# First phase of a hybrid decoder trunk: a 128-byte spacer, the vectors on ScalarE's queue, products pass by pass

## The chip, the core and the metric

The kernel runs on one core of one Trainium2 chip. The metric is the device time of one execution in microseconds; several executions are timed and their median is given. The engines of the core work side by side, each through a queue of its own, and wait for each other by semaphores: TensorE (PE) multiplies, VectorE (DVE) and ScalarE (ACT) do elementwise work, GpSimd (POOL) fills constants here, and SyncE (SP) issues nearly all DMAs.

## What is computed

Two layers over a sequence of 1024 tokens of width 1024: a gated linear recurrence (RG-LRU), a dense SwiGLU block, stick-breaking attention, and a second SwiGLU block. The change touches the beginning of the first mixer alone:

```python
def rms_norm(x, g):
    y = xf * lax.rsqrt(jnp.mean(xf * xf, axis=-1, keepdims=True) + RMS_EPS)
    return (y * g.astype(jnp.float32)).astype(x.dtype)
...
u = jnp.einsum("bsd,de->bse", x, w_in) + b_in
gate_branch, rec = u[..., :LRU_WIDTH], u[..., LRU_WIDTH:]
rec = causal_depthwise_conv(rec, conv_w, conv_b)
gl = jnp.einsum("bsnc,gncd->gbsnd", rec_blk, gate_w).reshape(2, bsz, seq, LRU_WIDTH)
```

## The kernel before

Activations lie transposed: 128 features by 512 tokens make a tile, so x is eight slices `d` (`ND`) by two halves `n` (`NH`). Each float32 operand is split into a rounded high part and a rest (`xh`, `xl`; `fh`, `fl`; `whi`, `wlo`), and a product is three passes: high by high, weight-high by low, weight-low by high. `mm3` (L638 to L641) issues the three, one line each.

The **first phase** (L738 to L829) makes four output columns of 128 (`FIRST`: the recurrent columns 8, 9, 10 and the gate column 0) from eight weight slices of 128 by 512. For each k it loads `fr[k]` and `xr[k][0]`, makes `fh`, `fl` (the weights' parts) and `xh`, `xl` (x times the norm's gain, which is a column of the small table `vc`), and runs twelve products, column after column, with three passes each. So 96 products follow for the first half of the tokens. The second half's 96 come from `second(i, ...)`, one column at a time: column 0, then four short products for the norm's sums (L597), then columns 1, 2 and 3. Column 3 with slice k = 7 is the last product of the phase, and it reads `fl7`.

The order of instructions in this phase is that of the code, on all five engines. Ahead of the first product PE runs ten small products of `ident` with itself (L774). On the DMA side, ScalarE's queue carries the first slice of x, and SP's carries `vc`, then `fr0`, `fr1`, `xr1` and so on. ACT's first computing instruction is `x_hi(0, 0)` (L758), in front of which a table is loaded.

**SBUF.** The pool `sp` holds, one behind the other, `fh0` to `fh7`, `fl0` to `fl7` (2048 bytes of a partition each), `sacc0`, `sacc1`, three `sq` and the raw tiles. It is closed at the end of the phase, and the pool `lp` of the recurrence starts at the same byte: `y0` to `y7` of 4096 bytes each, then two buffers `u` of 4160 bytes, then the rest. Both pools are opened with `reuse_waits="tile"`: whoever writes a new tile waits for the last user of the old tiles that lay on its bytes. Weights and x are apart: `xh`, `xl` begin 128 bytes behind a multiple of 256, and the `sp` pool at a multiple of 256.

**PSUM.** `ptile` (L730) hands out eight banks in turn. The first phase holds all eight (four columns by two halves), so the ninth product group, the first of the recurrence, takes the bank of the first column's first half.

The **recurrence** follows from L832 on. Its order on PE, ACT and DVE comes from a planner with costs of its own, and it is the same in both kernels. Its DVE work begins with `u_pad(0)` (L911: three columns of `u` in front, from `nbias`) and `u_half` (L914: `u` from a bank times the norm's factor `rbc`), for two columns; then a weight's low part (L888), the convolution's taps into `rec` (L923), its low part `rl` (L967), a chain of small instructions for the decay (L848 to L871), and the second `rl`. Its PE work begins with 48 products of `xh`, `xl` with `whi`, `wlo` into two banks, and then the gates' products of `rh`, `rl` into `g_ps` (L897 to L907). DVE and PE both take their instructions strictly in the order shown by the program's rows.

Of the kernel before, what the change touches and what calls it, by code (L numbers as in the profile page):

```python
# [9 lines left out]
F32 = mybir.dt.float32  # L10
# [3 lines left out]
AF = mybir.ActivationFunctionType  # L14
# [3 lines left out]
P = 128  # L18
S = 1024
D = 1024  # L20
ND = D // P
# [11 lines left out]
FIRST = (ND, ND + 1, ND + 2, 0)  # L33
# [471 lines left out]
def trunk(  # L505
# [15 lines left out]
    nc = tc.nc  # L521
# [37 lines left out]
    ones = cp.tile([P, 1], F32, name="ones")  # L559
    nc.gpsimd.memset(ones, 1.0)  # L560
    vc = cp.tile([P, P], F32, name="vc")
    tiny = cp.tile([P, 64], F32, name="tiny")
# [4 lines left out]
    xh, xl = [None] * ND, [None] * ND  # L567
# [43 lines left out]
    def all_factors(sums):  # L611
        for step in ("root", "square", "newton", "out"):
            for t in sums:
                getattr(t, step)()
# [23 lines left out]
    def mm3(ps, wh, wl, mh, ml, first, last, **kw):  # L638
        nc.tensor.matmul(ps, lhsT=wh, rhs=mh, start=first, stop=False, **kw)  # L639
        nc.tensor.matmul(ps, lhsT=wh, rhs=ml, start=False, stop=False, **kw)  # L640
        nc.tensor.matmul(ps, lhsT=wl, rhs=mh, start=False, stop=last, **kw)  # L641
# [88 lines left out]
    def ptile(name):  # L730
        turn[0] += 1
        return psl.tile([P, NB], F32, tag=f"a{(turn[0] - 1) % 8}", name=name)

    pa = {j: [ptile("a_ps") for n in range(NH)] for j in FIRST}
# [3 lines left out]
    with ExitStack() as st, tc.manual_schedule(engines={E.PE, E.Activation, E.DVE, E.Pool, E.SP}):  # L738
        sp = st.enter_context(tc.tile_pool(name="sp", bufs=1, reuse_waits="tile"))
        one = lambda name, dt=F32: sp.tile([P, NB], dt, tag=name, name=name)  # L740
        fh = [one(f"fh{k}", F32R) for k in range(ND)]
        fl = [one(f"fl{k}", F32R) for k in range(ND)]
        sacc = [one(f"sacc{n}") for n in range(NH)]
        sq = [one(f"sq{n}") for n in range(3)]
        fr = [one(f"fr{k}") for k in range(ND)]
        xr = [[one(f"xr{d}_{n}") for n in range(NH)] for d in range(ND)]
        f4 = lambda t: t.rearrange("p (t c) -> p t c", t=4)
        nc.scalar.dma_start(xr[0][0], x[0, 0])
        nc.sync.dma_start(vc, table)
        for k in range(ND):  # L750
            nc.sync.dma_start(f4(fr[k]), lru_first[k])
            if k:
                nc.sync.dma_start(xr[k][0], x[k, 0])
        for k in range(ND):
            nc.sync.dma_start(xr[k][1], x[k, 1])

        def x_hi(k, n):
            nc.scalar.activation(xh[k][n], xr[k][n], AF.Copy, scale=vc[:, V_MIX + k : V_MIX + k + 1])  # L758

        def x_lo(k, n):  # L760
            nc.vector.scalar_tensor_tensor(
                xl[k][n], xr[k][n], vc[:, V_MIX + k : V_MIX + k + 1], f32(xh[k][n]), op0=ALU.mult, op1=ALU.subtract
            )

        def x_square(k, n):
            nc.scalar.square(sq[k % 3] if k else sacc[n], xr[k][n])

        def x_add(k, n):
            if k:
                nc.vector.tensor_add(sacc[n], sacc[n], sq[k % 3])  # L770

        bank = pa[FIRST[3]][1]
        for i in range(10):
            nc.tensor.matmul(bank[:, 0:P], lhsT=ident, rhs=ident, start=True, stop=True)  # L774
        for k in range(ND):
            (nc.scalar.copy if k else V.tensor_copy)(fh[k], fr[k])
            x_hi(k, 0)
            x_square(k, 0)
            nc.vector.tensor_sub(fl[k], fr[k], f32(fh[k]))
            x_lo(k, 0)  # L780
            if k:
                x_add(k - 1, 0)
            for t, j in enumerate(FIRST):
                c = slice(t * P, (t + 1) * P)
                mm3(pa[j][0], fh[k][:, c], fl[k][:, c], xh[k][0], xl[k][0], k == 0, k == ND - 1)
        x_add(ND - 1, 0)
        for k in range(ND):
            x_hi(k, 1)
            x_lo(k, 1)
        for k in range(ND):  # L790
            x_square(k, 1)
            x_add(k, 1)

        def second(i, ks):
            for k in ks:
                c = slice(i * P, (i + 1) * P)
                mm3(pa[FIRST[i]][1], fh[k][:, c], fl[k][:, c], xh[k][1], xl[k][1], k == 0, k == ND - 1)

        again = lambda k, dt=F32: sp.tile([P, NB], dt, tag=f"fr{k}", name="again")
        sums = [  # L800
            Factors(sacc[n], again(n, F32R), again(2 + n, F32R), pa[FIRST[3 - n]][1], rbc[n], again(4 + n), rbc[n])
            for n in range(NH)
        ]
        sums[0].hi()
        sums[0].lo()
        second(0, range(ND))
        sums[1].hi()
        sums[1].lo()
        for t in sums:
            t.sums()  # L810
        all_factors(sums)
        sm = lambda name: lc.tile([P, ND], F32, name=name)
        lam = vc[:, V_LAM : V_LAM + ND]
        az, kq, gq, pq, cc, ch = (sm(n) for n in ("az", "kq", "gq", "pq", "cc", "ch"))
        cb = sm("cb")
        nbias = lc.tile([P, ND, 4], F32, name="nbias")
        cw = lambda j: vc[:, V_CW + j * ND : V_CW + (j + 1) * ND]
        bin_rec = vc[:, V_BIN + ND : V_BIN + 2 * ND]
        V.tensor_add(cb, cw(0), cw(1))
        V.tensor_add(cb, cb, cw(2))  # L820
        V.tensor_add(cb, cb, cw(3))
        V.tensor_mul(cb, cb, bin_rec)
        V.tensor_add(cb, cb, vc[:, V_CB : V_CB + ND])
        for j in range(3):
            V.tensor_scalar_mul(nbias[:, :, j], bin_rec, -1.0)
        V.tensor_scalar_mul(tiny[:, 32 : 32 + ND], vc[:, V_FIN : V_FIN + ND], -0.5)
        second(1, range(ND))
        second(2, range(ND))
        second(3, range(ND))  # L829
# [1444 lines left out]
```

## Time and profile before

| | us |
|---|---|
| median of 3 runs | 2161.24 |
| lowest, highest | 2160.73, 2161.38 |
| span of the profiled execution, first to last instruction | 2159.4 |
| median less span (start and end around the instructions; the profiled execution's own total is not listed) | 1.8 |
| DVE busy, share of the span | 1715.8, 79% |
| ACT busy, share of the span | 1099.4, 51% |

The page is of one execution. Its first part gives each engine's busy time; the groups give a line's instructions with mean durations; the timeline gives start, duration, engine, line and tiles of each instruction, and in brackets how long its engine had been idle and what ended that. Starts are microseconds from the first instruction. A product of 128 by 512 takes longer than the distance to the next one, since products overlap: the distance between two starts is what a product costs.

### The profile page before, as it was taken

What the parts mean: (1) busy time and instruction counts of PE and PEld (TensorE: products, weight loads), DVE (VectorE), ACT (ScalarE), POOL (GpSimd) and SP (SyncE); (2) the same over time, 40 slices, a digit from 0 to 9 for tenths busy, and PEclk for the clock granted to TensorE, in tenths of its full rate; (3) what the DMA queues carried; (4) which work ended last, traced back from release to release, by engine and by line L of the source; (5) the groups of instructions that cost most, each with busy time, mean ns of one, the idle gap of its engine ahead of it and who ended that gap; (6) DMA issues with size and microseconds to landing.
All of it is one profiled execution on the core that took longest, in us unless ns stands there. A gap on an engine that the chain in (4) does not pass through costs nothing.

```text
span 2159.4 us, 27027 instructions
## 1 busy us (share of the span) xinstructions
PE 2148.2 (99%) x9954; PEld 1781.6 (83%) x9954; DVE 1715.8 (79%) x2416; ACT 1099.4 (51%) x1793; POOL 29.2 (1%) x40
## 2 busy tenths in 40 slices
PE   9999999999999999999999999999999999999998
PEld 7888888888888888878888888888888888888887
DVE  8978678667777887888888888877967777787887
ACT  6677445344444544565555555544534444454555
POOL 0000020000000000000000000002000000000000
PEclk9999999999999999999999999999999999999999
DMA  4111312344444764444333334532133444467452
GB/s 177 39 49 49 127 39 84 100 139 146 133 160 136 276 198 122 147 141 103 100 97 96 101 88 107 167 139 95 59 117 125 145 140 151 141 233 243 130 161 86
DMA packets 133316, 274.61 MB, mean 127 GB/s; under 512 B 15296, under 2 KB 23872, under 8 KB 133184
## 3 DMA queue, kind: packets, MB, share of 16 engines
q1 hardware_dynamic: 132768, 272.36, 39.6%
q8 instruction: 78, 1.28, 0.2%
q10 hardware_dynamic: 416, 0.52, 0.1%
q14 instruction: 54, 0.44, 0.1%
HBM read 176.88 MB, written 70.78 MB: 115 GB/s over the span
## 4 chain that ended last, share of the span: by engine, by line
PE 96%; DVE 2%; ACT 1%; issue 0%; DMA 0%; POOL 0%; SPq 0%; DVEq 0%; ACTq 0%; POOLq 0%
PE p_ps L641 18%; PE p_ps L639 18%; PE p_ps L640 18%; PE qk_ps L639 4%; PE qk_ps L641 4%; PE qk_ps L640 4%; PE z_ps L2073 3%; PE av_ps L2121 3%; PE wt_ps L2104 3%; PE a_ps L640 3%; PE a_ps L641 3%; PE a_ps L639 3%; PE ob_ps L639 2%; PE ob_ps L640 2%; PE ob_ps L641 2%; PE g_ps L641 1%
## 5 line engine op out<-in xcount | busy, mean ns | idle before, releaser
L639 PE MATMUL p_ps<-vh,wbh 128*128 128x512 f32 x524 | 204.0, 389 | 1.2 <-ACT ta L1738 1.2
L641 PE MATMUL p_ps<-vh,wal 128*128 128x512 f32 x524 | 204.2, 390 | 0.5 <-DVE wal L1133 0.3
L641 PE MATMUL p_ps<-vh,wbl 128*128 128x512 f32 x524 | 204.1, 390 | 0.0
L641 PE MATMUL p_ps<-vh,wcl 128*128 128x512 f32 x524 | 204.0, 389 | 0.0
L639 PE MATMUL p_ps<-vh,wch 128*128 128x512 f32 x524 | 203.9, 389 | 0.0
L640 PE MATMUL p_ps<-vl,wah 128*128 128x512 f32 x524 | 203.9, 389 | 0.0
L640 PE MATMUL p_ps<-vl,wbh 128*128 128x512 f32 x524 | 203.9, 389 | 0.0
L639 PE MATMUL p_ps<-vh,wah 128*128 128x512 f32 x524 | 203.9, 389 | 0.0
L640 PE MATMUL p_ps<-vl,wch 128*128 128x512 f32 x524 | 203.8, 389 | 0.0
L1138 ACT CAST wbh<-sb 128x1024 fp32r<-128x1024 f32 (+2 forms) x69 | 69.8, 1011 | 191.3 <-DVE sb L1122 191.3
L2085 ACT ACTIVATE F<-z_ps 128x512 f32<-128x512 f32 (+3 forms) x188 | 92.1, 490 | 97.6 <-PE z_ps L2073 95.8
L2109 ACT CAST th<-wt_ps 128x512 fp32r<-128x512 f32 x192 | 92.3, 481 | 84.4 <-PE wt_ps L2104 78.1
L2092 DVE TENSOR_TENSOR_SCAN F<-F,unit 128x128 f32<-128x128 f32 (+3 forms) x128 | 104.9, 821 | 33.4 <-ACT F L2085 32.2
L2113 DVE TENSOR_TENSOR tl<-wt_ps,th 128x512 fp32r<-128x512 f32 x192 | 104.9, 546 | 16.6 <-ACT th L2109 16.5
L641 PEld LDWEIGHTS p_ps<-vh,wal 128*128 128x128 f32 x524 | 98.4, 188 | 22.0 <-DVE wal L1133 1.8
L639 PEld LDWEIGHTS p_ps<-vh,wbh 128*128 128x128 f32 x524 | 98.4, 188 | 21.9 <-ACT ta L1738 1.6
L641 PEld LDWEIGHTS p_ps<-vh,wbl 128*128 128x128 f32 x524 | 98.4, 188 | 21.2 <-DVE wbl L1142 0.8
L641 PEld LDWEIGHTS p_ps<-vh,wcl 128*128 128x128 f32 x524 | 98.4, 188 | 20.7 <-DVE wcl L1152 0.4
L640 PEld LDWEIGHTS p_ps<-vl,wbh 128*128 128x128 f32 x524 | 98.4, 188 | 20.5
L640 PEld LDWEIGHTS p_ps<-vl,wah 128*128 128x128 f32 x524 | 98.4, 188 | 20.5
L639 PEld LDWEIGHTS p_ps<-vh,wch 128*128 128x128 f32 x524 | 98.4, 188 | 20.5
L640 PEld LDWEIGHTS p_ps<-vl,wch 128*128 128x128 f32 x524 | 98.4, 188 | 20.5
(436 smaller groups left out, 5496.4 us busy)
## 6 DMA issues: line engine op xcount, KB each, us to landing
raw<-in_ffn_w_in SPq DMA_DIRECT2D x88, 512.0 KB, 3.6
vl<-pd SPq DMA_DIRECT2D x128, 256.0 KB, 3.5
pd<-U SPq DMA_DIRECT2D x90, 256.0 KB, 2.3
raw<-in_ffn_w_out SPq DMA_DIRECT2D x28, 512.0 KB, 4.1
raw<-in_attn_w_qkv SPq DMA_DIRECT2D x24, 512.0 KB, 3.8
kh<-qh SPq DMA_DIRECT2D x64, 128.0 KB, 2.3
kl<-ql SPq DMA_DIRECT2D x64, 128.0 KB, 2.3
acc<-pd SPq DMA_DIRECT2D x28, 256.0 KB, 2.6
```

Of the source, the lines that this page charges most:

```text
L639: nc.tensor.matmul(ps, lhsT=wh, rhs=mh, start=first, stop=False, **kw)
L640: nc.tensor.matmul(ps, lhsT=wh, rhs=ml, start=False, stop=False, **kw)
L641: nc.tensor.matmul(ps, lhsT=wl, rhs=mh, start=False, stop=last, **kw)
L1138: nc.scalar.copy(self.full(self.wb), self.full(self.sb))
L2073: nc.tensor.matmul(ps[:, 0:n], lhsT=lhsT, rhs=rhs, start=i == 0, stop=i == 1)
L2085: nc.scalar.activation(F, Z.pop(c)[:, 0:n], AF.Sigmoid, scale=-SC)
L2092: V.tensor_tensor_scan(rev, rev, unit[:, NB - n :][:, ::-1], 0.0, op0=ALU.mult, op1=ALU.add)
L2104: nc.tensor.transpose(tp[:, c : c + P], F[:, (kb % 4) * P : (kb % 4 + 1) * P], ident)
L2109: nc.scalar.copy(WH[u][:, c:], TP[u][:, c:])
L2113: V.tensor_sub(WL[u][:, c:], TP.pop(u)[:, c:], f32(WH[u])[:, c:])
L2121: nc.tensor.matmul(ps[:, c:], lhsT=VV[q][:, kb, hx], rhs=t.pop(u)[:, c:], start=kb == 4 * G and i == 0, stop=kb == 3 and i == 1,)
```

## The change

Four things change in the first phase. A tile `bent` of 32 floats (128 bytes of a partition) is put in front of `fh0` in the pool `sp` and filled with zeros by GpSimd; nothing reads it. The table `vc` is loaded from ScalarE's queue behind the first slice of x, and no longer from SP's queue. ScalarE then makes one element per partition of `tiny` from `ones` by `AF.Copy`; nothing reads that either. And the twelve products of a slice are issued pass by pass: high by high for all four columns, then weight-high by low for all four, then weight-low by high.

```diff
+        bent = sp.tile([P, P // 4], F32, name="bent")
+        nc.gpsimd.memset(bent, 0.0)
         fh = [one(f"fh{k}", F32R) for k in range(ND)]
         fl = [one(f"fl{k}", F32R) for k in range(ND)]
...
         nc.scalar.dma_start(xr[0][0], x[0, 0])
-        nc.sync.dma_start(vc, table)
+        nc.scalar.dma_start(vc, table)
+        nc.scalar.activation(tiny[:, 59:60], ones, AF.Copy, scale=ones)
...
-            for t, j in enumerate(FIRST):
-                c = slice(t * P, (t + 1) * P)
-                mm3(pa[j][0], fh[k][:, c], fl[k][:, c], xh[k][0], xl[k][0], k == 0, k == ND - 1)
+            for i, (w, m) in enumerate(((fh, xh), (fh, xl), (fl, xh))):
+                for t, j in enumerate(FIRST):
+                    nc.tensor.matmul(
+                        pa[j][0], lhsT=w[k][:, t * P : (t + 1) * P], rhs=m[k][0],
+                        start=k == i == 0, stop=k == ND - 1 and i == 2,
+                    )
```

Line numbers behind the phase grow by three to six. In the rows below, `DMAHW..` is the landing of a DMA, and `PE_49`, `DVE_49`, `Activation_49`, `Pool_49` are the engines' own counters.

The first place is ACT's queue at the very start, before:

```order
L748 DMA xr0_0_189<-in_x 128x512
L758 ACT_TABLE_LOAD [waits DMAHW1_49]
L758 ACTIVATE xh0_0_93<-xr0_0_189,vc_80 128x512 [waits DMAHW0_49]
L766 ACTIVATE sacc0_176<-xr0_0_189 128x512
L776 CAST fh1_161<-fr1_182 128x512 [waits DMAHW3_49]
```

and in the changed kernel:

```order
L750 DMA xr0_0_191<-in_x 128x512
L751 DMA vc_80<-in_table 128x128
L752 ACT_TABLE_LOAD
L752 ACTIVATE tiny_81<-ones_78 128x1 [waits Pool_49]
L761 ACTIVATE xh0_0_93<-xr0_0_191,vc_80 128x512 [waits DMAHW2_49,DMAHW0_49]
L769 ACTIVATE sacc0_178<-xr0_0_191 128x512
```

The table load stood behind the wait for `vc`; now it waits for nothing, and `x_hi(0, 0)` has both waits for its data.

The second place is PE at the first slice, behind the ten products of `ident`, before:

```order
L639 MATMUL a_ps_144<-xh0_0_93,fh0_160 128x512 [waits DVE_49,Activation_49]
L640 MATMUL a_ps_144<-xl0_0_109,fh0_160 128x512 [waits DVE_49]
L641 MATMUL a_ps_144<-xh0_0_93,fl0_168 128x512
L639 MATMUL a_ps_146<-xh0_0_93,fh0_160 128x512
L640 MATMUL a_ps_146<-xl0_0_109,fh0_160 128x512
```

and in the changed kernel:

```order
L788 MATMUL a_ps_144<-xh0_0_93,fh0_162 128x512 [waits DVE_49,Activation_49]
L788 MATMUL a_ps_146<-xh0_0_93,fh0_162 128x512
L788 MATMUL a_ps_148<-xh0_0_93,fh0_162 128x512
L788 MATMUL a_ps_150<-xh0_0_93,fh0_162 128x512
L788 MATMUL a_ps_144<-xl0_0_109,fh0_162 128x512 [waits DVE_49]
```

The product that needs `xl0` was the second and is now the fifth.

The third place is DVE at the seam to the recurrence, where `u_583` (`u_586` in the changed kernel) is the recurrence's first buffer `u`, and `a_ps_144` to `a_ps_147` are the banks of the first phase's columns 0 and 1. Before:

```order
L826 TENSOR_SCALAR tiny_81<-vc_80 128x8
L911 COPY u_583<-nbias_467 128x3 [waits DVE_49]
L914 TENSOR_TENSOR u_583<-a_ps_144,rbc0_83 128x512 [waits PE_49]
L914 TENSOR_TENSOR u_583<-a_ps_145,rbc1_84 128x512 [waits PE_49]
L911 COPY u_587<-nbias_467 128x3
L914 TENSOR_TENSOR u_587<-a_ps_146,rbc0_83 128x512
L914 TENSOR_TENSOR u_587<-a_ps_147,rbc1_84 128x512 [waits PE_49]
L888 TENSOR_TENSOR wlo_577<-raw_568,whi_576 128x1024 [waits DMAHW3_49]
```

and in the changed kernel:

```order
L832 TENSOR_SCALAR tiny_81<-vc_80 128x8
L917 COPY u_586<-nbias_470 128x3 [waits DVE_49,PE_49]
L920 TENSOR_TENSOR u_586<-a_ps_144,rbc0_83 128x512
L920 TENSOR_TENSOR u_586<-a_ps_145,rbc1_84 128x512
L917 COPY u_590<-nbias_470 128x3
L920 TENSOR_TENSOR u_590<-a_ps_146,rbc0_83 128x512
L920 TENSOR_TENSOR u_590<-a_ps_147,rbc1_84 128x512
L894 TENSOR_TENSOR wlo_580<-raw_571,whi_579 128x1024 [waits DMAHW3_49]
```

The order is the same, but the first copy into `u` now waits for PE, and the multiplications behind it no longer do.

## Prediction

> **What bounds the kernel now.** I read the page's first part and its chain first.
>
> ```profile
> span 2159.4 us, 27027 instructions
> PE 2148.2 (99%) x9954; PEld 1781.6 (83%) x9954; DVE 1715.8 (79%) x2416; ACT 1099.4 (51%) x1793; POOL 29.2 (1%) x40
> PE 96%; DVE 2%; ACT 1%; issue 0%; DMA 0%; POOL 0%; SPq 0%; DVEq 0%; ACTq 0%; POOLq 0%
> ```
>
> PE is never idle for long, and the chain that ended last is PE for 96% of the span. So whatever PE gains or loses in the first phase stands at the end unless PE waits for something later that did not move with it; all later work hangs on PE, directly or through DVE. Averages say no more than that: the change must be read at its own place. The timeline of the first 8 us:
>
> ```profile
> 0.74 0.40 SPq L749 DMA_DIRECT2D vc<-in_table  x1
> 0.74 0.41 ACTq L748 DMA_DIRECT2D xr<-in_x  x1
> 0.87 0.10 POOL L560 MEMSET ones<- 128x1 f32 x1
> 0.91 0.10 POOL L563 MEMSET tiny<- 128x1 f32 x1
> 1.19 0.90 SPq L751 DMA_DIRECT2D fr<-in_lru_first  x2
> 1.45 4.63 PE L774 MATMUL a_ps<-ident 128*128 128x128 f32 x20 [1.45 <-POOL ident masks.py:199]
> 3.68 1.28 ACT L758 ACT_TABLE_LOAD   x1 [3.68 <-DMA vc<-in_table]
> 4.57 0.43 DVE L776 CAST fh<-fr 128x512 fp32r<-128x512 f32 x1 [3.34 <-DMA fr<-in_lru_first]
> 4.97 0.72 ACT L758 ACTIVATE xh<-xr,vc 128x512 fp32r<-128x512 f32 x1
> 5.75 0.80 PE L639 MATMUL a_ps<-xh,fh 128*128 128x512 f32 x1
> 6.53 0.29 PEld L640 LDWEIGHTS a_ps<-xl,fh 128*128 128x128 f32 x1 [0.50 <-DVE xl L761]
> 6.99 0.73 ACT L758 ACTIVATE xh<-xr,vc 128x512 fp32r<-128x512 f32 x1 [0.27 <-DMA xr<-in_x]
> 7.12 0.55 PE L641 MATMUL a_ps<-xh,fl 128*128 128x512 f32 x1
> 7.51 0.40 PE L639 MATMUL a_ps<-xh,fh 128*128 128x512 f32 x1
> ```
>
> The table load waits for `vc` and then holds `xh` until 4.97. The first product starts at 5.75, where the small `ident` products end as well, and the second waits 0.50 for `xl`. Products take 0.80 at first and 0.40 from 7.51 on: PE runs at half rate until about 7.4, that is for 6.0 us from its first instruction at 1.45.
>
> Next, what a product costs, from starts in PE's timeline in this phase and behind it (the last row is of the view by windows; its last two numbers are the share of the DMA engines and GB/s):
>
> ```profile
> 34.57 0.40 PE L641 MATMUL a_ps<-xh,fl 128*128 128x512 f32 x1
> 35.97 0.39 PE L640 MATMUL a_ps<-xl,fh 128*128 128x512 f32 x1
> 52.24 0.40 PE L641 MATMUL a_ps<-xh,fl 128*128 128x512 f32 x1
> 52.47 0.39 PE L639 MATMUL a_ps<-xh,whi 128*128 128x512 f32 x1
> 64.04 0.39 PE L639 MATMUL g_ps<-rh,whi 128*128 128x512 f32 x1
> 64.27 0.39 PE L640 MATMUL g_ps<-rl,whi 128*128 128x512 f32 x1
> 72.88 0.39 PE L639 MATMUL g_ps<-rh,whi 128*128 128x512 f32 x1
> 36.00:52.40 16.40, 16.40 (x72) 13.32 (x71) 13.53 (x26) 6.66 (x8) 0.00 (x0) 1.00 0.10 33
> ```
>
> From 7.51 to 34.57 there are 116 distances, 0.2333 us each; from 35.97 to 52.47 there are 71, 0.2324 each; from 52.47 to 64.27, in the recurrence, 52 of 0.2269. So the first phase's products, whose weights and x lie 128 bytes apart modulo 256, cost 0.006 more than the recurrence's, where they lie alike.
>
> Last, DVE at the seam to the recurrence:
>
> ```profile
> 42.27 0.17 DVE L911 COPY u<-nbias 128x3 f32<-128x3 f32 x1
> 42.34 1.28 DVE L914 TENSOR_TENSOR u<-a_ps,rbc 128x512 f32<-128x512 f32 x2
> 43.60 1.28 DVE L914 TENSOR_TENSOR u<-a_ps,rbc 128x512 f32<-128x512 f32 x2
> 44.80 1.22 DVE L888 TENSOR_TENSOR wlo<-raw,whi 128x1024 fp32r<-128x1024 f32 x1
> 45.94 6.44 DVE L923 SCALAR_TENSOR_TENSOR rec<-u,vc,rec 128x1024 f32<-128x1024 f32 x5
> 52.29 1.22 DVE L967 TENSOR_TENSOR rl<-rec,rh 128x1024 fp32r<-128x1024 f32 x1
> 53.43 1.28 DVE L923 SCALAR_TENSOR_TENSOR rec<-u,vc,rec 128x1024 f32<-128x1024 f32 x1
> 54.62 0.16 DVE L848 SCALAR_TENSOR_TENSOR az<-vc 128x8 f32<-128x8 f32 x1
> 61.17 1.22 DVE L967 TENSOR_TENSOR rl<-rec,rh 128x1024 fp32r<-128x1024 f32 x1
> 71.54 0.68 DVE L914 TENSOR_TENSOR u<-a_ps,rbc 128x512 f32<-128x512 f32 x1
> ```
>
> None of these rows carries an idle time in brackets: from 42.27 on DVE works without a hole, ten microseconds ahead of the end of PE's phase at 52.24 plus 0.40. PE uses that work soon: the second `rl` ends at 62.39 and is read by the product at 64.27, 1.9 us later; the multiplication that ends at 72.22 frees the bank that the product at 72.88 writes, 0.65 later. These two are the cover that DVE has.
>
> **The change part by part.** The sums are made in the time of this execution (span 2159.4, which lies 1.8 below the median of 2161.24; that rest is taken as unchanged).
>
> *Start.* `vc` goes out on ACT at about 1.19, where `fr0` goes out now. `fr0` was used at 4.57, so by that row `vc`, which is smaller but shares the engines with two slices, is there at about 4.6; the ends are 4.0 (2.9 after issue, as `vc` took on SP's queue: 0.74 to 3.68) and 6.4 (the 5.2 that the later slices took, by the rows of DMA issues below). With the table loaded meanwhile, `xh` takes 0.72 and ends near 5.3. PE gains nothing there: it is in its small products until 5.75. I take 5.75 for the first product; the later end of `vc` would make it 7.2. The spacer's fill on POOL stands ahead of `ident`: POOL's fills start 0.04 apart, so it moves PE's small products by 0.03 to 0.1.
>
> ```profile
> fr<-in_lru_first SPq DMA_DIRECT2D x7, 256.0 KB, 5.2
> vc<-in_table SPq DMA_DIRECT2D x1, 64.0 KB, 2.9
> ```
>
> *Pass by pass.* Four products need only `xh` and `fh`, so the 0.50 wait for `xl` goes. But PE is at half rate there: a product there costs between 0.39 (7.12 to 7.51, in which the rate changed) and twice 0.2267; I take 0.43. Three products from 5.75, the first of 0.59 with its weights (as from 6.53 to 7.12), bring the fourth to 7.2, where it was 7.51. Gain 0.3, between 0 and 0.5. Later slices have their data long before PE comes to them (`xh` of slice 1 ends at 7.72; PE comes to it twelve products after 5.75, behind 9), so the order of passes does nothing more.
>
> *Spacer, on products.* It brings weights and x to the same place modulo 256, as in the recurrence. At 0.2269, 116 distances give 0.74 and 71 give 0.39: with the few left out, 1.2 in all. The bounds are 0 and this.
>
> The Trainium skill ("TensorE: Matmul & The Clock Gate", section "Step-by-step: what each phase is for") says that PE reads weights and moving data through two independent SBUF ports, so that loading weights takes nothing from a running product. By it the spacer would bring 0 and the sum would end 1.2 higher. The two distances above speak for the spacer, so I keep 1.2.
>
> So the last product of the phase starts at 52.24 - 0.3 - 1.2 = 50.8 and ends near 51.2.
>
> *Spacer, on memory: the term that decides.* `fh` and `fl` are sixteen times 2048 bytes, `y0` to `y7` eight times 4096: both 32768. So now `u` begins exactly where `sacc0` did, and its earlier owners are tiles that DVE itself used last. With 128 bytes in front, the last 128 bytes of `fl7` slide under `u`. `fl7` is read by the last product of the phase, so the copy into `u` has to wait for PE's last product; the order shows that this copy gains a wait for PE and that the multiplications behind it lose theirs, as behind a wait that covers them. The copy moves from 42.27 to about 51.25: DVE stands still for 9 us, and everything above moves by 9.0. ACT waits for these `u` too.
>
> PE then meets DVE three times. (a) The first product of the recurrence takes the bank that the first multiplication reads: done at 51.25 + 0.07 + 0.69 = 52.0, where PE would be at 51.0. PE waits 1.0. (b) 48 products later PE is at 62.9 and goes on with the first `rh`, `rl`; the second `rl` ends at 62.39 + 9.0 = 71.4. The product that stood at 64.27 starts at 71.45: 7.2 later than before, after 6.2 us of idle PE. (c) The multiplication at 71.54 moves to 80.5 and ends at 81.2; the product that stood at 72.88 starts at 81.25, though PE alone would be there at 80.05. That is 8.4 later than before: 9.0 of delay less the smallest cover of 0.65. Behind this point DVE, busy 79% of the span, can catch up, and nothing makes PE catch up, so 8.4 stays.
>
> *Half rate again.* The end of the trace shows what PE's clock does when it has nothing to do:
>
> ```profile
> 2152.29 0.28 PE L1583 MATMUL ob<-we,vl 128*128 128x256 f32 x1
> 2156.00:2157.80 1.80, 0.00 (x0) 0.00 (x0) 0.00 (x0) 0.00 (x0) 0.00 (x0) 1.00 1.03 343
> 2157.80:2159.40 1.60, 0.00 (x0) 0.00 (x0) 0.00 (x0) 0.00 (x0) 0.00 (x0) 0.51 0.01 3
> ```
>
> The granted clock falls to half at 2157.8, 5.2 us after the last product. The wait in (b) is 6.2, so I expect the fall within it, and then half rate for a while behind 71.45; at the start it lasted 6.0. Each product then costs 0.20 more (0.43 for 0.2269). At 6.0 us that is 14 products, 2.8; at 4.0 it is 9, 1.9. Of it 1.2 lies under the wait in (c), which PE no longer has to sit out. So 0.7 to 1.6 is added; I take 1.1 (5 us).
>
> Sum: 8.4 + 1.1 = 9.5, and 2161.24 + 9.5 = **2170.7**.
>
> The Trainium skill (same page, section "What's actually happening") says that the clock is judged in free-running windows of 3413 ns: one idle window halves it, one busy window restores it. This trace agrees: from 7.4 to 2157.8 are 630.0 such windows. By that rule a wait of 6.2 holds a whole idle window in about four executions of five, and the return takes 4 to 7 us, so executions would differ by 1 to 2 us among themselves.
>
> **Rivals.** *The clock doesn't fall* in the wait: 8.4, so 2169.6. For it: the trace shows one such fall only, and 6.2 is little more than its 5.2. *The spacer doesn't change the products' cost*: the phase ends 1.2 later, DVE and PE with it: 2171.9. For it: the first phase is also the one with the most DMA traffic and the busiest DVE, which could cost PE the 0.006; against it, the phase's second part costs 0.2324 at a DMA share of 0.10. *The wait is covered*: the new wait on the copy could stand only for the products that the multiplications waited for anyway, which are done by 42.3; or DVE's delay could stay below the cover. The deciding point is a start of the copy at 44.1 (42.27 plus 1.9, less little): ahead of it PE never waits, and the change brings its gains alone, 0.3 + 1.2: 2159.7, not slower. Against it stands the arithmetic of the bytes. *The start is late*: `vc` at 6.4 costs up to 1.4 less what half rate hides, so 2171.5 to 2172.
>
> **How the numbers follow.** Forecast 0.57, clock keeps 0.19, products keep their cost 0.10, late start 0.05, wait covered 0.09. The first four lie between 2168.5 (8.4 less an error of 0.4 in each of two covers, and 0.3 for the spread of runs) and 2172.8 (8.4, 1.6 for the clock, the spacer's 1.2 lost, and 0.3 again). The range is **2168.5 to 2172.8**; the covered wait at 2159.7 is left out with its 0.09. A measurement of this kernel tells about 0.2% (4.3 us) from no change: the first four are slower by more than that, the covered wait falls within it, and nothing in the change can bring 4.3. Faster 0.01, same 0.09, slower 0.90.
>
> **What would show it.** In the profile of the changed kernel: the distance of products in the first phase 0.227; the copy into `u` (L917) with some 9 us of idle time in brackets, released by PE at about 51; the product of the second `rl` near 71.5 with about 6 us of idle time, released by DVE L973; products of 0.8 us behind it if the clock fell; the wait for `vc` ended by 5.0. I am wrong if L917 starts near 42, or if PE has made up the delay by 100 us.

## The result, and the profile after

| | before | changed |
|---|---|---|
| median of 5 runs each, us | 2161.16 | 2172.82 |
| lowest, highest | 2160.73, 2161.38 | 2172.03, 2173.52 |
| span of the profiled execution | 2159.4 | 2170.4 |

The changed kernel is slower by 11.7 us: the ratio is 1.0053, with a 95% interval of 1.0042 to 1.0063. The forecast was 2170.7 with a range of 2168.5 to 2172.8, so the median lies at the range's upper bound, 0.02 beyond it as the figures stand. The profiled execution's own time is 2172.21, which is near the low end of the five.

The page of the changed kernel, its first part and its chain:

```profile
span 2170.4 us, 27031 instructions
PE 2149.7 (99%) x9954; PEld 1782.4 (82%) x9954; DVE 1715.7 (79%) x2416; ACT 1098.0 (51%) x1794; POOL 29.2 (1%) x41
PE 93%; DVE 3%; ACT 1%; DMA 1%; issue 1%; SPq 0%; DVEq 0%; ACTq 0%
```

The same number of products keeps PE busy for 1.5 us more, which cannot make 11. The chain shows where to look: PE's share falls from 96% to 93% and DVE's rises by a point, so a stretch has come in where PE is not what ends last. The waits of the changed kernel between 36 and 110 us, PE's first and then DVE's largest (the sum, how often, the longest):

```profile
PE g_ps L640 <- DVE rl L973: 6.1, 1, 6.1
PE g_ps L639 <- ACT rh L935: 0.9, 1, 0.9
PE a_ps L639 <- DVE u L920: 0.9, 1, 0.9
DVE u L917 <- PE a_ps L641: 10.3, 1, 10.3
```

Before the change PE had no wait there that the same view lists. Now the rows of the timeline behind these four, in order of time:

```profile
51.41 0.39 PE L641 MATMUL a_ps<-xh,fl 128*128 128x512 f32 x1
51.84 0.17 DVE L917 COPY u<-nbias 128x3 f32<-128x3 f32 x1 [10.29 <-PE a_ps L641]
52.66 0.50 PE L639 MATMUL a_ps<-xh,whi 128*128 128x512 f32 x1 [0.85 <-DVE u L920]
65.41 0.50 PE L639 MATMUL g_ps<-rh,whi 128*128 128x512 f32 x1 [0.89 <-ACT rh L935]
70.71 1.22 DVE L973 TENSOR_TENSOR rl<-rec,rh 128x1024 fp32r<-128x1024 f32 x1
71.98 0.80 PE L640 MATMUL g_ps<-rl,whi 128*128 128x512 f32 x1 [6.08 <-DVE rl L973]
72.58 0.63 PE L641 MATMUL g_ps<-rh,wlo 128*128 128x512 f32 x1
76.84 0.47 PE L639 MATMUL g_ps<-rh,whi 128*128 128x512 f32 x1
77.15 0.40 PE L640 MATMUL g_ps<-rl,whi 128*128 128x512 f32 x1
81.08 0.68 DVE L920 TENSOR_TENSOR u<-a_ps,rbc 128x512 f32<-128x512 f32 x1
```

A copy of three columns, 0.17 long, waits 10.29 us until the phase's last product (51.41 plus 0.39) is done. DVE's next work moves with it: the second `rl` from 61.17 to 70.71 and the multiplication from 71.54 to 81.08, both by 9.54. PE meets that delay at 71.98 after 6.08 idle, and the products behind stand 0.43 apart (72.58 to 76.84, ten distances) instead of 0.227. The view by windows shows the clock there (length, then busy time and count of PE, PEld, DVE, ACT, POOL, then the granted clock, DMA share and GB/s):

```profile
63.33:66.74 3.41, 1.69 (x7) 0.83 (x5) 3.00 (x14) 1.99 (x2) 0.00 (x0) 1.00 0.00 0
66.74:70.15 3.41, 0.00 (x0) 0.00 (x0) 2.83 (x18) 0.00 (x0) 0.00 (x0) 0.50 0.00 0
70.15:73.57 3.42, 1.59 (x4) 1.30 (x5) 3.35 (x9) 0.00 (x0) 0.00 (x0) 0.50 0.00 0
73.57:76.98 3.41, 3.41 (x10) 2.64 (x9) 3.41 (x6) 2.52 (x2) 0.00 (x0) 0.50 0.00 0
76.98:80.39 3.41, 3.41 (x17) 2.77 (x16) 3.34 (x4) 3.03 (x5) 0.00 (x0) 1.00 0.45 154
```

The clock is at half from 66.74 to 76.98, of which PE has work for the last 5.0 us.

To place the loss I use one measure throughout: the **lead**, the start of a product less the start of the same product before the change (a positive lead is late). In the changed kernel it is -0.83 at the phase's last product (51.41 against 52.24), 7.71 at the product of `rl` (71.98 against 64.27), 10.20 when the kernel before stands at 78 us, and 10.66 at the last product of all. So nearly all of the loss arises within 26 us.

The beginning came out unlike the forecast:

```profile
1.20 0.45 ACTq L751 DMA_DIRECT2D vc<-in_table  x1
1.67 1.28 ACT L752 ACT_TABLE_LOAD   x1 [1.67 <-PEq L2268]
4.34 0.43 DVE L779 CAST fh<-fr 128x512 fp32r<-128x512 f32 x1 [3.11 <-DMA fr<-in_lru_first]
5.42 0.72 ACT L761 ACTIVATE xh<-xr,vc 128x512 fp32r<-128x512 f32 x1 [2.15 <-DMA vc<-in_table]
6.19 1.20 PE L788 MATMUL a_ps<-xh,fh 128*128 128x512 f32 x4 [0.39 <-ACT xh L761]
7.22 1.07 PE L788 MATMUL a_ps<-xl,fh 128*128 128x512 f32 x4
```

The table is loaded early, as meant, but then ACT stands idle for 2.15 us until `vc` has landed. The first product starts at 6.19, 0.44 later than before. The four products of `xl` wait for nothing.

### The profile page after: what moved, and what is told of

Same layout as the page of the kernel before. It is cut to its first block, busy times and chain, and to the rows that moved or that the text cites. A ratio compares the mean times of both kernels' runs of the same rounds, so it can differ in the third digit from the quotient of the medians.

```text
span 2170.4 us, 27031 instructions
## 1 busy us (share of the span) xinstructions
PE 2149.7 (99%) x9954; PEld 1782.4 (82%) x9954; DVE 1715.7 (79%) x2416; ACT 1098.0 (51%) x1794; POOL 29.2 (1%) x41
## 3 DMA queue, kind: packets, MB, share of 16 engines
q8 instruction: 78, 1.28, 0.2%
## 4 chain that ended last, share of the span: by engine, by line
PE 93%; DVE 3%; ACT 1%; DMA 1%; issue 1%; SPq 0%; DVEq 0%; ACTq 0%
PE p_ps L641 18%; PE p_ps L639 18%; PE p_ps L640 18%; PE qk_ps L639 4%; PE qk_ps L641 4%; PE qk_ps L640 4%; PE z_ps L2079 3%; PE av_ps L2127 3%; PE wt_ps L2110 3%; PE ob_ps L639 2%; PE ob_ps L640 2%; PE ob_ps L641 2%; PE a_ps L639 2%; PE a_ps L640 2%; PE a_ps L641 2%; PE g_ps L640 1%
```

## The experiments

The theory was: the 128 bytes push the end of `fl7` under the recurrence's first `u`, so a copy on DVE waits for PE's last product; that wait, and half rate behind it, are the whole loss. The rivals were a late start (through `vc`), the pass order, and the spacer's effect on PE itself. Eleven kernels ran, in three groups; each is compared with the kernel before in runs of its own group.

| kernel | median, us | runs | before | ratio, 95% interval | lead at 52, at 78, at the end |
|---|---|---|---|---|---|
| `e1_u_moved` | 2161.53 | 11 | 2161.35 | 1.0001 [0.9992, 1.0010] | -0.59, -0.61, 0.39 |
| `e2_spacer_alone` | 2171.25 | 5 | 2161.35 | 1.0046 [1.0033, 1.0058] | -1.28, 8.97, 9.31 |
| `e3_no_spacer` | 2161.32 | 11 | 2161.35 | 1.0001 [0.9992, 1.0010] | -0.37, -0.34, -0.52 |
| `e4_spacer_u_moved` | 2160.57 | 11 | 2161.35 | 0.9997 [0.9988, 1.0006] | -1.32, -1.34, -0.75 |
| `e5_vc_on_sp` | 2161.04 | 11 | 2161.23 | 0.9999 [0.9990, 1.0008] | -1.38, -1.37, -0.27 |
| `e8_spacer_256` | 2161.46 | 10 | 2161.23 | 1.0001 [0.9992, 1.0010] | -0.16, -0.15, 0.63 |
| `e6_pe_busy` | 2172.86 | 4 | 2161.23 | 1.0055 [1.0041, 1.0069] | -0.76, 9.19, 10.99 |
| `e7_after_again` | 2172.25 | 4 | 2161.23 | 1.0053 [1.0039, 1.0067] | -0.69, 10.13, 10.49 |
| `e10_pe_busy_24` | 2172.44 | 5 | 2161.22 | 1.0051 [1.0039, 1.0064] | -0.82, 9.09, 10.73 |
| `e11_after_third` | 2172.68 | 5 | 2161.22 | 1.0052 [1.0040, 1.0065] | -0.98, 10.00, 10.31 |
| `e9_spacer_64` | 2160.77 | 10 | 2161.22 | 0.9999 [0.9989, 1.0008] | -1.25, -1.25, -0.96 |

**Is it the bytes under `u`?** The changed kernel with 128 bytes put in front of the first `u` and 128 behind the second, so that `u` begins where `sacc0` did and the rest on a multiple of 256. The products and the start are unchanged.

```diff
+        lp.tile([P, 32], F32, name="gap0")
...
+            if len(U) == 2:
+                lp.tile([P, 32], F32, name="gap1")
```

> The changed kernel, with 128 bytes left free between the y buffers and the u buffers (and 128 more behind the two u, so that everything behind keeps its place modulo 256): u no longer lies on fl7. Theory (the wait of the copy into u for the phase's last product costs the time): the copy starts near 41 without a wait, PE never waits 6 us, the clock stays full, and of the changed trace only the lead of about 0.85 us at the phase's end is left: 2160.3 us. Rival (the cost lies in the new order of passes, in the start or in the moved table vc): 2170 us or more. Rival (only the clock's half rate costs, the wait itself is covered): about 2169.

The copy in the timeline of this kernel:

```profile
41.73 0.17 DVE L920 COPY u<-nbias 128x3 f32<-128x3 f32 x1
```

No idle time stands in brackets, the view of waits lists none for PE between 36 and 110 us, and the 11 us are gone: 2161.53 against 2172.82 (runs of different groups; the kernel before agrees within 0.2 in them). The wait is the cause. The gain that should have been left, about 1 us, is not there: the lead is only -0.59 at the phase's end, and later waits use it up.

**Does the spacer do it alone?** The kernel before with `bent` and its fill, and nothing else.

```diff
+        bent = sp.tile([P, 32], F32, name="bent")
+        nc.gpsimd.memset(bent, 0.0)
```

> The kernel before with the 128-byte spacer and its fill alone. Theory: products of the first phase at 0.227 us, the copy into u waits about 10 us for PE, PE waits about 6 us for the second rl: as slow as the changed kernel, 2172 to 2173.5 us. Rival (pass order and start carry the cost): close to the time before, 2160 to 2161.2.

```profile
51.38 0.17 DVE L913 COPY u<-nbias 128x3 f32<-128x3 f32 x1 [10.22 <-PE a_ps L641]
```

PE's longest wait in it between 36 and 110 us:

```profile
PE g_ps L640 <- DVE rl L969: 6.1, 1, 6.1
```

The same waits, and 9.9 us of loss (2171.25 less 2161.35). So neither the queue of `vc` nor the pass order is needed for it. The median lies 0.75 under the range that was expected. Two differences of its trace from that of the changed kernel point the same way: the copy stands at 51.38, 0.46 earlier, and half rate ends at 74.91, 2.1 earlier.

**And the rest without the spacer?** The changed kernel without `bent`.

```diff
-        bent = sp.tile([P, P // 4], F32, name="bent")
-        nc.gpsimd.memset(bent, 0.0)
```

> The changed kernel without the spacer: vc on ScalarE's queue, the early table load and the order pass by pass are left. Theory: no wait of the copy for PE, products at 0.233 us, first product near 6.2 and the wait for xl gone: a lead of about 0.5 us, of which the norm's sums may take a part: 2160.6 to 2161.2 us. Rival (these parts carry the cost): 2165 us or more.

It takes as long as the kernel before. Its first product also starts at 6.19, the distance of products stays at 0.2333 from 35.54 to 51.87, and up to 100 us the lead never goes beyond -0.62. The median lies 0.1 above the range that was expected. The other edits together are worth nothing that can be measured.

**What the spacer is worth without its wait.** The kernel before with `bent`, `gap0` and `gap1`.

> The kernel before with the spacer, and with u moved away from fl7 as in e1. Theory: the spacer's gain alone, 187 products 0.006 us cheaper, 1.2 us, of which up to 0.5 is given back where the norm's sums wait for DVE: 2160.0 to 2160.5 us. Rival (the lower cost of products came from something else than the spacer): products at 0.233 and 2161.2 us.

PE's first and last products of the phase's second part in this kernel (70 distances):

```profile
35.04 0.39 PE L640 MATMUL a_ps<-xl,fh 128*128 128x512 f32 x1
50.92 0.39 PE L641 MATMUL a_ps<-xh,fl 128*128 128x512 f32 x1
```

(50.92 - 35.04) / 70 = 0.2269, where the kernel before had 0.2324. The lead of -1.32 is not the spacer's alone: -0.27 stands at the fourth product already. From there to the norm's sums it goes to -1.04, 0.11 is lost at the sums, and behind them it goes from -0.93 to -1.32. So the products themselves bring 1.16, the 1.2 that the prediction took for them, and the lead lasts until later waits take half. The median is 0.8 us lower, the lowest of the eleven kernels, but the interval of the ratio holds 1.

**Is it the place of the weights modulo 256, or any displacement?** The kernel before with a spacer of 256 bytes, `gap0` of 256 and no `gap1`; then one with a spacer of 64 bytes, `gap0` of 64 and `gap1` of 192.

```diff
+        bent = sp.tile([P, 64], F32, name="bent")
+        nc.gpsimd.memset(bent, 0.0)
...
+        lp.tile([P, 64], F32, name="gap0")
```

> The kernel before with a spacer of 256 bytes and u moved by as much: everything lies elsewhere, but weights and x are 128 bytes apart modulo 256 as before. Theory (the place modulo 256 sets a product's cost): products of the first phase at 0.233, 2161.2 to 2161.5 us. Rival (any shift or the added tile helps): 0.227 and about 2160.5 us, as e4.

> The kernel before with a spacer of 64 bytes, and the places behind the weights made up to 256 bytes so that u and the tiles behind it lie as before. Weights and x then stand 64 bytes apart in a window of 256 (128 in the kernel before, 0 with the 128-byte spacer). If any distance but 0 costs, products keep their 0.233 us and the first phase is as long as before (lead within 0.2 us at 50 us). If only 128 costs, the pitch is 0.227 and the lead at 50 us is 1.2 to 1.4 us. Total 2160.5 to 2161.6 either way.

With 256 bytes the products cost the same as before, (52.08 - 35.81) / 70 = 0.2324, and the lead stays at -0.14 to -0.16 from the fourth product to the phase's last:

```profile
35.81 0.39 PE L640 MATMUL a_ps<-xl,fh 128*128 128x512 f32 x1
52.08 0.40 PE L641 MATMUL a_ps<-xh,fl 128*128 128x512 f32 x1
```

With 64 bytes, weights and x then 64 apart, they cost 0.2290 (34.96 to 50.99):

```profile
34.96 0.40 PE L640 MATMUL a_ps<-xl,fh 128*128 128x512 f32 x1
50.99 0.40 PE L641 MATMUL a_ps<-xh,fl 128*128 128x512 f32 x1
```

So what counts is where the weights lie modulo 256, and not that something was displaced: 128 apart costs 0.0055 a product more than 0 apart, and 64 apart 0.002, between the two outcomes that had been set down. No run moved x, so the distance between weights and x and the place of the weights by itself are not told apart. The lead of -1.25 with 64 bytes looks as large as that of `e4_spacer_u_moved`, but 0.50 of it is there at the fourth product already (0.27 there), from a start that differs from run to run.

**What `vc` on ScalarE's queue costs.** `e1_u_moved` with `vc` back on SP's queue; table load and pass order stay.

```diff
-        nc.scalar.dma_start(vc, table)
+        nc.sync.dma_start(vc, table)
```

> As e1 (the whole change, u moved off fl7), but with vc back on SP's queue ahead of the first weights. Theory (vc behind x on ScalarE's queue lands late, near 5.4, and sets the first product at 6.2 to 6.4): xh starts near 3.9, the first product at 5.8 where PE's small products end, and the time is 0.4 to 1.0 us under e1: 2160.3 to 2161.0. Rival (the late start is hidden by the norm's sums): the same as e1, 2161.5.

The beginning of this kernel:

```profile
3.91 0.72 ACT L761 ACTIVATE xh<-xr,vc 128x512 fp32r<-128x512 f32 x1 [1.14 <-DMA xr<-in_x]
5.80 1.87 PE L788 MATMUL a_ps<-xh,fh 128*128 128x512 f32 x4
```

`xh` starts 1.5 us sooner than with `vc` on ScalarE's queue (5.42). The median of 2161.04 lies 0.5 under that of `e1_u_moved`, which ran in another group; both intervals hold 1, so the times alone don't tell the two apart. The other price is at the norm's sums. The waits of the changed kernel between 28 and 37 us hold a row that the kernel with `vc` on SP's queue doesn't have:

```profile
PEld a_ps L597 <- DVE again L593: 1.2, 2, 0.7
```

ACT starts its chain of squares later, so `again` is later (33.45 against 32.61), and the sums on PE wait for it: from the last product ahead of the sums to the second behind them it is 2.25 us (33.29 to 35.54), against 1.38 here and 1.40 before. So the new place of `vc` takes back some 0.85 of what the spacer had gained by then.

**Is half rate a term of its own?** The changed kernel with products of `ident` by `ident` into the first gate's bank, ahead of its first product, so that PE is busy through most of its wait; 34 of them, then 24. Beside each the changed kernel itself ran once more.

```diff
+            for _ in range(34 if eg == (0, 0) and n == 0 else 0):
+                nc.tensor.matmul(PS[eg, n][:, 0:P], lhsT=ident, rhs=ident, start=True, stop=True)
```

> The changed kernel with 34 added products of ident with itself (128x128, overwritten by what follows) ahead of the first gate product, some 7 us of PE work at full rate in front of its long wait. Theory (the half rate behind the wait is part of the loss): PE's wait shrinks to below 1 us, the clock stays full, the wait for u's bank near 81.8 ends the delay instead: 1.2 to 1.8 us faster than the changed kernel, about 2171.2. Rival (the half rate lies under DVE's work and costs nothing): the same as the changed kernel, 2172.8. If the added products outlast the wait, 2173 or more.

> The changed kernel again, word for word, so that e6 has it on the same chip. Theory: 2172 to 2173.5 us, the clock at half rate for 7 to 10 us around the wait for the second rl.

> The changed kernel with 24 (not 34) idle products of ident by ident ahead of the first gate product. If the half rate after the wait is a term of its own of about 1 us, the clock stays at 1.00 from 60 to 84 us, the product that used to wait for the second rl starts at about 72.0, the lead lost by 78 us is 9.0 to 9.3 us instead of the 10.2 of the changed kernel, and the median is about 1 us under that of the changed kernel in the same call (about 2171.8 against 2172.8). Rival: the median stays within 0.4 us of the changed kernel's, as with 34 products; then what the clock gives back early is lost again at the later waits for transfers (980, 1533, 2010 us), which would be seen as steps of the lead there.

> The changed kernel once more, beside the kernel with the 24 products: 2172.0 to 2173.5; clock at half rate for two or three stretches of 3.41 us after 66 us; lead lost by 78 us 10.1 to 10.3 us, by the end 10.4 to 10.7.

The windows of the kernel with 24, and its wait for the second `rl`:

```profile
63.70:70.00 6.30, 6.30 (x53) 5.90 (x51) 5.34 (x31) 1.99 (x2) 0.00 (x0) 1.00 0.00 0
70.00:73.00 3.00, 1.11 (x5) 0.86 (x5) 2.90 (x8) 0.00 (x0) 0.00 (x0) 1.00 0.00 0
73.00:77.00 4.00, 4.00 (x19) 3.15 (x18) 4.00 (x8) 2.53 (x2) 0.00 (x0) 1.00 0.01 4
```

```profile
PE g_ps L640 <- DVE rl L975: 1.9, 1, 1.9
```

The clock stays full in both, and the lead at 78 us is 9.19 and 9.09, against 10.20, 10.13 and 10.00 in three traces of the changed kernel. At its place half rate costs 0.8 to 1.1 us in the changed kernel. In `e2_spacer_alone` it costs less: half rate ended at 74.91, after 3.4 us of PE's work. Set against the delay of the copy, since that differs between traces, the lead at 78 us is 0.45 and 0.49 less with full clock, 0.42 to 0.63 more in the changed kernel, and 0.15 less in `e2_spacer_alone`, so some 0.3 there. But the totals did not follow: 2172.86 against 2172.25 with 34 products, where 1.2 to 1.8 us less was expected, and 2172.44 against 2172.68 with 24, where about 1 us less was. The steps of the lead show where it went. Around 980 us a product waits for a transfer, in the kernel with 34:

```profile
PE z_ps L2081 <- DMA kl<-ql: 1.2, 1, 1.2
```

In the kernel before this wait is 0.2. There the lead grows by 0.99 and 0.76 in the two kernels with full clock, and by 0.27, 0.24 and 0.48 in the three traces with half rate. A second such place is at about 2010 us: 0.45 and 0.59 are lost there with full clock, and 0.05, 0.22 and 0.47 are won with half rate. The two places together take back more than the whole gain. Why they fall out so was not found, and with so few traces it can be chance; the runs of one of these kernels also lie 0.7 to 3.1 us apart.

## Why the prediction was right, point by point

*The copy waits for PE's last product, and the spacer's 128 bytes do it.* Right: with the bytes moved the wait is gone (`e1_u_moved`), and the spacer alone brings it (`e2_spacer_alone`). The rival of a covered wait fell with the first trace. Only the size was a little small: the copy was put at 51.25 and came at 51.84, so DVE lost 9.54 instead of 9.0.

*The start.* This is the term that had the wrong sign, when what it does at the norm's sums is counted in: a gain of 0.3 was forecast, and 0.52 gained at the fourth product less 0.85 lost at the sums is a loss of 0.33. `vc` was to be there at 4.6; it was used at 5.42 (the bounds were 4.0 and 6.4), so the first product came 0.44 later and not at 5.75. The 0.50 wait for `xl` went, as forecast. In this trace the clock was also full from 5.30 on, where it was from 7.44 before, so the fourth product started at 6.99 instead of 7.51 in spite of the late start. The record of the clock begins at these times; before them the length of the products tells of half rate. Whether the change has a part in that is open: the clock became full between 4.5 and 5.8 in the seven traces with `vc` on ScalarE's queue, and between 5.4 and 7.4 in the other six. That the fourth product came earlier than forecast is luck, as far as anything here shows. "The order of passes does nothing more" held. That a late `vc` also reaches the sums through ACT, for 0.85, was not in the prediction at all; less the 0.2 by which the fourth product beat its forecast (-0.5 instead of -0.3), it is the 0.6 by which the copy was late.

*The spacer on products.* Right: 0.2267 from 35.54 to 51.41, and 0.2269 in `e4_spacer_u_moved`; without spacer, or with 256 bytes, the old distance. The rival that products keep their cost is out. The Trainium skill's rule of two independent ports ("TensorE: Matmul & The Clock Gate", section "Step-by-step: what each phase is for") would have given 0 here; the measured 0.0055 a product speaks against it for these operands. No run shows why the place costs, or that it is the loading of weights that costs it.

*PE meets DVE three times.* (a) 0.85 idle, forecast 1.0. (b) 6.08 idle and 71.98, forecast 6.2 and 71.45; a wait of 0.89 for `rh` just ahead of it, at 65.41, was not foreseen and cost nothing beside it, since the product of `rl` could not start sooner. (c) With half rate PE did not have to wait, as the prediction had it; with full clock it did, 0.9, and the lead was 9.1: the 9.54 of delay less 0.65 of cover is 8.9, where the forecast had 8.4.

*Half rate again.* The fall came, in every trace with that wait unfilled (four of four, `e2_spacer_alone` among them), so the rival that the clock stays is out. PE worked at half rate for 5.0 us, as taken, and the cost at the place is 0.8 to 1.1, the 1.1 of the sum (in `e2_spacer_alone`, with 3.4 us of such work, some 0.3). What it adds to the total could not be told from nothing, as said above.

The sum by the trace: 8.9 and 1.3 (in this trace: 10.20 - 8.9) by 78 us, 0.46 at later waits, 0.34 between the last product and the end, which is the 11.0 of the spans; the profiled execution lies 0.6 under its median. The forecast's 9.5 lacked 0.7 in the first 78 us, mostly the late copy, and counted nothing behind it. It had said that behind that point nothing makes PE catch up; it also held that nothing more is lost, which is not so by half a microsecond. The range left little room for that: the terms of its upper bound add up to 2172.74.

## What to carry to other kernels

Ahead of moving a tile in a pool whose bytes a later pool takes over, write down for each later tile which old tile will then lie under it and who used that last: here 128 bytes cost 11 us, because the tile newly beneath is last read by PE, ten microseconds after DVE was ready to write there. The price of such a wait is the delay of the waiting engine less the smallest time by which its later results are ahead of their use; here that gave 8.9, and half rate and later waits came on top. An edit with several parts is worth taking apart: its one part of value, the spacer, came to 0.8 us under the kernel before once 128 bytes more kept `u` in its place, which these runs could not tell from nothing.

## What the runs showed of the hardware

A product's cost depends on where its weights lie in a window of 256 bytes of a partition, with x always at one place: 0.2324 to 0.2333 us at 128 bytes apart, 0.2290 at 64, 0.2267 to 0.2269 at 0.

The clock falls without an idle stretch of its own. It steps at intervals of 3.41 us (half rate lasted 10.24 here, three of them, and 6.83 in `e2_spacer_alone`, two). The stretch from 63.33 to 66.74 had PE busy for 1.69 of 3.41 and was followed by half rate; the one from 70.15 to 73.57, busy for 1.59, did not bring the full clock back. In `e7_after_again` a stretch with 2.16 busy kept it:

```profile
62.99:66.40 3.41, 2.16 (x9) 1.23 (x7) 3.07 (x13) 1.96 (x2) 0.00 (x0) 1.00 0.00 0
66.41:69.82 3.41, 0.00 (x0) 0.00 (x0) 2.87 (x18) 0.03 (x1) 0.00 (x0) 1.00 0.00 0
```

So for the fall about half a stretch of work decides, and the end of the kernel before, where 1.56 kept the full clock, says that the bound is not a sharp one in busy time. The rise takes more: in the kernel before, PE was busy with its small products for 2.58 of the 3.41 us up to 4.03, and the products of 0.80 behind that show half rate still; in `e1_u_moved` 3.01 busy up to 4.52 was enough. The Trainium skill ("TensorE: Matmul & The Clock Gate", section "What's actually happening") asks for one idle window of 3413 ns; the length agrees, but by that rule the clock would have stayed until 70.15 here. Where in its stretch a wait begins differs from execution to execution, and with it when half rate begins: 66.74, 69.82 and 69.93 in three traces of the changed kernel.

The same small transfer can take longer to be there: `vc` was used 4.2 us after its issue as the second on ScalarE's queue (1.20 to 5.42), against 2.9 as the first on SP's queue (0.74 to 3.68). Whether the queue, the second place in it or the larger transfers beside it make the difference, no run tells.
